# Reordering the first step of a Strassen-Winograd MLP: an operand split ahead of the up products, other roundings behind a copy

## The chip, the cores and the metric

The kernel runs on one core of a Trainium2 chip. The metric is device microseconds for one execution, the median of several runs. The core's engines are named PE (TensorE, the matmuls), ACT (ScalarE), DVE (VectorE), POOL (GpSimd) and SP (SyncE, which issues most DMAs). Each works through its own list of instructions in order; semaphores tie the lists together.

## The reference

A trunk of two layers on 512 tokens of width 1024. Layer 0 mixes with multi-head latent attention, layer 1 with gated linear attention; behind each stands an MLP of hidden width 4096 with a squared ReLU. The change touches the MLPs alone:

```
def sq_relu_mlp(xn, w_up, w_down):
    hid = jnp.square(jax.nn.relu(xn @ w_up))
    return hid @ w_down

x = x + sq_relu_mlp(rms_norm(x, norm_mlp[i]), w_up[i], w_down[i])
```

All values are float32, x is 512x1024, w_up 1024x4096 and w_down 4096x1024.

## The kernel before, in words

**Products in three matmuls.** To keep float32 accuracy every operand is split into a high part, rounded to the format that PE multiplies at full speed (an ACT instruction), and a low part, the rest (a DVE instruction): `split`, lines 124 and 127; with a sign, `signed`, lines 870 and 871. A product is then high x high, high x low and low x high. Tiles `wh` and `wl` are the parts of weights and rotate over four buffers each.

**The MLP.** `mlp` is called once per layer; `nxt` is set in the first MLP (a norm follows) and empty in the second. The hidden width is cut into eight blocks of 512. `up_first` makes the first block with plain products. Then seven calls of `step(b, ...)` follow, each of which makes the next hidden block (up) and adds the present one to the result (down). Both are 2x2 block products done with seven instead of eight quadrant products (Strassen-Winograd), so sums and differences of quadrants have to be formed first: of x once (`quadrants`, tiles T), of the weights in each step (in place, tiles `wraw` and `comb`, or by an accumulating DMA of POOL), of the hidden block in each step (`q11` to `q22`). A hidden block's quadrants lie in tiles that the trace calls `set`; their parts lie in `hidden_parts` in the first MLP and in `set` tiles in the second. There are four rooms for such parts (`parts_room`), used in turn.

**One step in its order on PE.** Up: products named by their x operand, "11" into bank z, T1 into w, T2 onto z, "21" onto y, T3 onto z, "22" onto w, T4 onto z. Between them ACT copies banks: y is a copy of z behind "11" (T2 may overwrite z only then), w2 a copy of w behind T1, u a copy of z behind T2, v a copy of z behind T3. `finish` (lines 885 and 886) applies ReLU and square to a finished quadrant. Down: d11 into the pair of banks d, whose sum ACT copies to the pair e; then d22, d12 (onto e), d11 again (onto d), dS1, d12, dS3. A product `onto` a total starts by copying ("seeding") the total from SBUF into two `u` banks. Up products are line 993; down products are line 1006 in the first MLP and line 1013 in the second.

**The operands of the down products.** In step 0, before the change: q11 is split ahead of the up products (`p11`). Behind the copy e of d11 in the source come, in this order, q12 = q22 - q12 (L1067), q11 = q11 + q12 (L1068), the parts of q21 (`p21`, for the first d12), q21 = q21 - q11 (L1070) and its negated parts (for d22), then the negated parts of the new q11 (for the second d11), and the parts of q22 (`p22`, for the second d12).

**The totals.** The residual stream itself serves as the totals S11, S12, S21 and SU. `residual` prepares it: in the first MLP it negates SU in place (L931, ACT) and forms the difference S21 (L932, DVE); in the second it first turns the tiles by transpositions on PE (L941) through d and e, which ACT copies out (L945, L946, L948) before DVE forms S21 (L949). The third transposition needs the bank that L945 frees.

**What sets the order.** The Tile framework orders each engine's instructions by its own estimate of when they can run, from the order in the source and the dependencies; `tc.issue_after(i)` keeps instructions behind instruction i, and `tc.keep_in_program_order` keeps one at its place in the source.

Of the kernel before, what the change touches and what calls it, by code (L numbers as in the profile page):

```python
# [14 lines left out]
AF = mybir.ActivationFunctionType  # L15
ALU = mybir.AluOpType
# [34 lines left out]
def trunk_kernel(ctx: ExitStack, tc: tile.TileContext, t_in: dict, out: bass.AP):  # L51
    nc = tc.nc
    PE, ACT, DVE, POOL, SP = nc.tensor, nc.scalar, nc.vector, nc.gpsimd, nc.sync
# [5 lines left out]
    def uname(s):  # L59
        count[0] += 1  # L60
        return f"{s}_{count[0]}"
# [17 lines left out]
    def two_banks(tag):  # L79
        return psum["pool"].tile([P, 1024], F32, tag=f"ps_{tag}", bufs=1, name=uname("ps2"))  # L80
# [8 lines left out]
    def tmp(shape=(P, 512), dt=F32):  # L89
        return sb.tile(list(shape), dt, tag="tmp", bufs=6, name=uname("tmp"))  # L90
# [739 lines left out]
    def mlp(layer, nrm, nxt=None):  # L830
# [20 lines left out]
        if nxt:  # L851
            S11, S12, S21, SU = (xall[:, c * KH : (c + 1) * KH, t] for c in range(2) for t in (first, second))
        else:
            S11, S12, SU, S21 = (xall[:, 2 * i : 2 * i + 2].rearrange("p a t -> p (a t)") for i in range(4))
# [18 lines left out]
        def parts_of_quad(src, sign=1.0):  # L873
            hi, lo = parts_room[turn[0] % 4]
            turn[0] += 1
            if sign == 1.0:
                split(src, hi, lo)
            else:
                signed(src, hi, lo, sign)
            return hi, lo  # L880

        def finish(src, half, th, q):
            r = tmp()
            r_t = nrm.rstd[:, (first, second)[th]].unsqueeze(1).to_broadcast([P, 2, TH])
            DVE.scalar_tensor_tensor(by_tile(r), by_tile(src), 0.0, r_t, ALU.min if half else ALU.max, ALU.mult)
            ACT.activation(q[half][th], r, AF.Square)
# [40 lines left out]


        def residual():
            if nxt:  # L930
                ACT.activation(SU, SU, AF.Copy, scale=-1.0)  # L931
                DVE.scalar_tensor_tensor(S21, S21, -1.0, SU, ALU.mult, ALU.subtract)  # L932
                return

            def turned(tag, c, th):
                p = two_banks(tag)
                for t in range(2):
                    for j in range(4):
                        o = t * 512 + j * P
                        src = xT[4 * c + j][:, th * TH + t * P : th * TH + (t + 1) * P]  # L940
                        PE.matmul(p[:, o : o + P], src, ident, start=j == 0, stop=j == 3, is_transpose=True, skip_group_check=True)  # L941
                return p

            p, q = turned("d", 0, 0), turned("e", 0, 1)
            ACT.activation(S11, p, AF.Copy)  # L945
            ACT.activation(S12, q, AF.Copy)  # L946
            p, q = turned("d", 1, 1), turned("e", 1, 0)
            ACT.activation(SU, p, AF.Copy, scale=-1.0)  # L948
            DVE.scalar_tensor_tensor(S21, q, -1.0, SU, ALU.mult, ALU.subtract)  # L949
# [66 lines left out]
        def step(b, q, r, after):  # L1016
            (q11, q12), (q21, q22) = q
            A1, A2, s1 = W["A1"], W["A2"], W["S1"]
            a11, a12, s3, a22 = A1[:, :KH], A1[:, KH:], A2[:, :KH], A2[:, KH:]
            d11, d12, ds1, ds3, d22 = (W[n] for n in ("d11", "d12", "dS1", "dS3", "d22"))  # L1020

            def copied(dst, src):
                ACT.activation(dst, src, AF.Copy)  # L1023
                return dst

            def onto(total, a, parts, fresh=False):
                pair = [bank("u"), bank("u")]
                cols = [part_of(total, i) for i in range(2)]
                if not fresh:
                    for p, c in zip(pair, cols):  # L1030
                        copied(laid(p), c)
                down_product(pair, a, parts, fresh)
                for p, c in zip(pair, cols):
                    copied(c, laid(p))

            p11 = None if b else parts_of_quad(q11)
            w, w2, z, y = (bank("u") for _ in range(4))
            up_product(z, a11, "11", True)
            copied(y, z)
            DVE.tensor_tensor(a11, s1, a11, ALU.add)  # L1040
            up_product(w, s1, "T1", True)
            copied(w2, w)
            after("S1")
            up_product(z, a11, "T2", False)
            u = copied(tmp(), z)
            up_product(y, a12, "21", False)
            finish(y, 0, 0, r)
            DVE.tensor_tensor(a12, a11, a12, ALU.add)
            up_product(z, s3, "T3", False)
            v = copied(tmp(), z)  # L1050
            c = tmp()
            DVE.tensor_tensor(c, w2, v, ALU.add)
            finish(c, 1, 1, r)
            up_product(w, a12, "22", False)
            c = tmp()
            DVE.tensor_tensor(c, w, u, ALU.add)
            finish(c, 0, 1, r)
            after("A1")
            up_product(z, a22, "T4", False)
            finish(z, 1, 0, r)  # L1060
            after("A2")

            d = two_banks("d")
            down_product(d, d11, p11 or parts_of_quad(q11), True)
            e = copied(two_banks("e"), d)
            DVE.tensor_tensor(d11, ds1, d11, ALU.add)
            DVE.tensor_tensor(q12, q22, q12, ALU.subtract)  # L1067
            DVE.tensor_tensor(q11, q11, q12, ALU.add)  # L1068
            p21 = parts_of_quad(q21)
            DVE.tensor_tensor(q21, q21, q11, ALU.subtract)  # L1070
            onto(S21, d22, parts_of_quad(q21, -1.0))
            after("d22")
            down_product(e, d12, p21, False)
            DVE.tensor_tensor(S11, laid(e), S11, ALU.add)
            down_product(d, d11, parts_of_quad(q11, -1.0), False)
            e = copied(two_banks("e"), d)
            DVE.tensor_tensor(d12, d11, d12, ALU.add)
            after("d11")
            p22 = parts_of_quad(q22)
            DVE.tensor_tensor(q22, q22, q11, ALU.subtract)  # L1080
            onto(S5, ds1, parts_of_quad(q22, -1.0), b == 0)
            after("dS1")
            down_product(e, d12, p22, False)
            DVE.tensor_tensor(S12, laid(e), S12, ALU.add)
            after("d12")
            down_product(d, ds3, parts_of_quad(q12), False)
            DVE.tensor_tensor(SU, laid(d), SU, ALU.add)
            after("dS3")

        up_first(Q[0])  # L1090
        quadrants()
        residual()
        for name in ("A1", "S1", "A2", "d11", "dS1", "d22", "d12", "dS3"):
            fetch(0, name)
        last_raw, last, gain = [], [[], []], []
# [43 lines left out]
        if nxt:  # L1139
# [7 lines left out]
            for c in range(2):  # L1147
                if c == 0:
                    ps_ = [bank("u") for _ in range(4)]
                else:  # L1150
                    e, d = split_banks("e"), split_banks("d")
# [541 lines left out]
    O, begun = mla(0, nrm, w0, mla_pools)  # L1693
# [25 lines left out]
    Y, begun = gla(0, n_mix1, "B", "B")  # L1719
# [54 lines left out]
```

## Time and profile before

| | |
|---|---|
| median of 3 runs | 1041.1 us (1040.84 to 1041.17) |
| the profiled execution | 1041.6 us, its span 1039.9 us |
| DVE busy / ACT busy | 878.8 us (85%) / 695.8 us (67%) |
| granted PE clock | 0.998 |
| first step of the first MLP | 206.0 to 245.1 us of the span |
| first step of the second MLP | 740.4 to 782.5 us |

The span runs from the first to the last instruction of the profiled execution; the execution's own time contains 1.7 us around it. Rows of a timeline give start and duration in us, engine, line of the source, operation, output and input tile (numbers left out), shapes, a count if several were merged, and in brackets the idle time of the engine before it with what ended it. Rows of windows give the stretch, its length, and for each engine its busy time and, in brackets, the number of instructions; then the granted clock, the share of time in which the DMA engines worked, and GB/s.

### The profile page before, as it was taken

The page shows a single profiled execution, that of the slowest core. Times are in us where ns is not written, and L with a number is a line of the kernel's source. Part 1 is how long each engine was busy: PE and PEld are TensorE (multiplying, and loading weights), DVE is VectorE, ACT ScalarE, POOL GpSimd, SP SyncE. Part 2 cuts the span into 40 slices and gives each one's busy share as a digit, 9 for nine tenths or more (in the row PEclk, how much of TensorE's full clock was granted, in tenths as well). Part 3 has the DMA queues.
Part 4 walks back from the last instruction along what each step waited for, and adds up shares of the span by engine and source line. Part 5 has one row for each costly group of instructions (what it writes and reads, how often), then busy time and mean ns, then how long its engine had stood idle before and what let it go on. Part 6 is the DMA issues. An engine that isn't in the chain of part 4 may idle for free.

```text
span 1039.9 us, 16853 instructions
## 1 busy us (share of the span) xinstructions
PE 1028.7 (99%) x6522; PEld 922.0 (89%) x6522; DVE 878.8 (85%) x1343; ACT 695.8 (67%) x1130; POOL 113.6 (11%) x128
## 2 busy tenths in 40 slices
PE   9999999999999999999999999999999999999997
PEld 7788888899999999998888888888989989989986
DVE  7889976999989989989686499469699999898994
ACT  8667754586776876775345565655577687677785
POOL 7400000411111111000000000000001101111000
PEclk9999999999999999999999999999999999999999
DMA  7401214788788778623313212164678778778522
GB/s 234 123 21 41 82 41 151 194 203 197 188 204 203 182 200 204 146 82 122 91 41 95 95 55 82 50 160 150 151 185 197 177 208 198 188 195 191 121 82 82
DMA packets 120001, 145.85 MB, mean 140 GB/s; under 512 B 9488, under 2 KB 86288, under 8 KB 119920
## 3 DMA queue, kind: packets, MB, share of 16 engines
q1 hardware_dynamic: 95424, 113.57, 34.2%
q0 software_dynamic: 22400, 29.36, 18.1%
q10 hardware_dynamic: 2096, 1.84, 0.6%
q8 instruction: 51, 0.84, 0.3%
q14 instruction: 30, 0.25, 0.1%
HBM read 142.39 MB, written 2.10 MB: 139 GB/s over the span
## 4 chain that ended last, share of the span: by engine, by line
PE 88%; DVE 5%; ACT 3%; DMA 2%; issue 1%; SPq 0%; ACTq 0%; DVEq 0%
PE ps L993 26%; PE ps L1013 13%; PE ps L1006 12%; PE ps L132 10%; PE ps L134 10%; PE ps L133 10%; PE ps L1413 1%; PE ps L149 1%; PE ps L1193 1%; DVE wl L127 1%; DMA wraw<-in_mla_w_in_dram 1%; PE ps L1540 1%; ACT wh L124 1%; DVE acc L266 1%; PE ps L1159 1%
## 5 line engine op out<-in xcount | busy, mean ns | idle before, releaser
L124 ACT ACTIVATE wh<-wraw 128x1024 fp32r<-128x1024 f32 x139 | 146.3, 1056 | 118.5 <-issue 39.7
L127 DVE TENSOR_TENSOR wl<-wraw,wh 128x1024 fp32r<-128x1024 f32 x139 | 169.7, 1222 | 38.4 <-ACT wh L124 37.7
L993 PE MATMUL ps<-T,wh 128*128 128x256 f32 x896 | 154.6, 275 | 0.6 <-ACT tmp L1023 0.6
L127 DVE TENSOR_TENSOR wl<-comb,wh 128x1024 fp32r<-128x1024 f32 x112 | 136.7, 1221 | 14.2 <-ACT wh L124 14.2
L124 ACT ACTIVATE wh<-comb 128x1024 fp32r<-128x1024 f32 x112 | 118.4, 1058 | 41.3 <-issue 31.4
L993 PEld LDWEIGHTS ps<-T,wh 128*128 128x128 f32 x896 | 134.7, 188 | 0.8 <-ACT tmp L1023 0.8
L1013 PE MATMUL ps<-wh,set 128*128 128x512 f32 x392 | 122.3, 390 | 1.4 <-ACT ps L1023 1.4
L993 PE MATMUL ps<-T,wl 128*128 128x256 f32 x448 | 123.3, 275 | 0.0
L993 PE MATMUL ps<-set,wh 128*128 128x256 f32 x672 | 116.7, 276 | 0.0
L132 PE MATMUL ps<-set,wh 128*128 128x512 f32 x280 | 109.5, 391 | 0.0
L133 PE MATMUL ps<-set,wh 128*128 128x512 f32 x280 | 109.5, 391 | 0.0
L134 PE MATMUL ps<-set,wl 128*128 128x512 f32 x280 | 109.3, 390 | 0.0
L1006 PE MATMUL ps<-hidden_parts,wh 128*128 128x256 f32 x784 | 105.9, 275 | 0.0
L993 PEld LDWEIGHTS ps<-set,wh 128*128 128x128 f32 x672 | 101.6, 188 | 0.5
L1006 PEld LDWEIGHTS ps<-hidden_parts,wh 128*128 128x128 f32 x784 | 96.7, 188 | 0.0
L993 PE MATMUL ps<-set,wl 128*128 128x256 f32 x336 | 92.6, 276 | 0.0
L1013 PEld LDWEIGHTS ps<-wh,set 128*128 128x128 f32 x392 | 73.6, 188 | 17.2 <-ACT ps L1023 1.8
L993 PEld LDWEIGHTS ps<-T,wl 128*128 128x128 f32 x448 | 84.1, 188 | 0.0
L1013 PE MATMUL ps<-wl,set 128*128 128x512 f32 x196 | 76.1, 389 | 0.0
L993 PEld LDWEIGHTS ps<-set,wl 128*128 128x128 f32 x336 | 63.1, 188 | 0.0
L134 PEld LDWEIGHTS ps<-set,wl 128*128 128x128 f32 x280 | 52.6, 188 | 11.2 <-DVE wl L127 0.2
L133 PEld LDWEIGHTS ps<-set,wh 128*128 128x128 f32 x280 | 52.6, 188 | 10.9 <-DVE set L765 0.2
(405 smaller groups left out, 2213.1 us busy)
## 6 DMA issues: line engine op xcount, KB each, us to landing
comb<-in_mlp_w_down_dram SPq DMA_DIRECT2D x74, 512.0 KB, 4.5
wraw<-in_mlp_w_up_dram SPq DMA_DIRECT2D x18, 1024.0 KB, 5.6
wraw<-in_mlp_w_up_dram SPq DMA_DIRECT2D x28, 512.0 KB, 5.8
comb<-in_mlp_w_down_dram POOLq DMA_DIRECT2D x28, 512.0 KB, 6.7
wraw<-in_gla_w_in_dram SPq DMA_DIRECT2D x12, 1024.0 KB, 5.2
comb<-in_mlp_w_up_dram SPq DMA_DIRECT2D x14, 512.0 KB, 4.7
comb<-in_mlp_w_up_dram POOLq DMA_DIRECT2D x14, 512.0 KB, 6.2
wraw<-in_mlp_w_up_dram POOLq DMA_DIRECT2D x14, 512.0 KB, 7.8
```

Of the source, the lines that this page charges most:

```text
L124: order(ACT.activation(hi, src, AF.Copy))
L127: lo_eng.tensor_tensor(lo, src, f(hi), ALU.subtract)
L132: PE.matmul(psum, wh, xh, start=start, stop=False)
L133: PE.matmul(psum, wh, xl, start=False, stop=False)
L134: PE.matmul(psum, wl, xh, start=False, stop=stop)
L149: PE.transpose(psum, src, ident[: src.shape[0], : src.shape[0]])
L266: DVE.tensor_tensor(self.acc, self.acc, s, ALU.add)
L993: PE.matmul(o, a_, x_, start=start and j == 0 and k == 0 and n == 0, stop=k == KH - 1 and n == 2, skip_group_check=True)
L1006: PE.matmul(o, w_[:, k, j * P : (j + 1) * P], x_[:, ts], start=opens, stop=k == 1 and n == 2, skip_group_check=True)
L1013: PE.matmul(o, x_, w_, start=start and k == 0 and n == 0, stop=k == 1 and n == 2, skip_group_check=True)
L1159: PE.matmul(p, a, x, start=k == 0 and n == 0, stop=k == 3 and n == 2)
L1193: PE.matmul(o, a, b_, start=False, stop=k == 3 and n == 2, skip_group_check=True)
```

## The change

Five edits, all in `mlp`. They concern step 0 alone (`b == 0`), and there differ between the two MLPs:

1. The parts of q21 (`p21`) are made ahead of the up products, behind those of q11.
2. In the second MLP the two sums of quadrants (`combined`) and the negated q21 with its parts (`negated`) are made there too.
3. In the second MLP the negated parts of q11 and the parts of q22 are issued behind the first copy e (`later`).
4. In the first MLP `residual` is no longer called before the steps; its two instructions stand in step 0 behind the sum for the "22" quadrant (lines 1067 and 1068 of the new file), the DVE one held at its place in the source.
5. The copy e of d11 is written out as `begun`, so that edit 3 can name it.

```diff
         def residual():
-            if nxt:
-                ACT.activation(SU, SU, AF.Copy, scale=-1.0)
-                DVE.scalar_tensor_tensor(S21, S21, -1.0, SU, ALU.mult, ALU.subtract)
-                return
...
-            p11 = None if b else parts_of_quad(q11)
+            def combined():
+                DVE.tensor_tensor(q12, q22, q12, ALU.subtract)
+                DVE.tensor_tensor(q11, q11, q12, ALU.add)
+
+            def negated():
+                DVE.tensor_tensor(q21, q21, q11, ALU.subtract)
+                return parts_of_quad(q21, -1.0)
+
+            p11, p21, m21 = None, None, None
+            if b == 0:
+                p11 = parts_of_quad(q11)
+                p21 = parts_of_quad(q21)
+                if not nxt:
+                    combined()
+                    m21 = negated()
...
             DVE.tensor_tensor(c, w, u, ALU.add)
+            if nxt and not b:
+                ACT.activation(SU, SU, AF.Copy, scale=-1.0)
+                tc.keep_in_program_order(DVE.scalar_tensor_tensor(S21, S21, -1.0, SU, ALU.mult, ALU.subtract))
             finish(c, 0, 1, r)
...
-            e = copied(two_banks("e"), d)
+            e = two_banks("e")
+            begun = ACT.activation(e, d, AF.Copy)
+
+            def later():
+                return nullcontext() if b or nxt else tc.issue_after(begun.ins)
+
             DVE.tensor_tensor(d11, ds1, d11, ALU.add)
-            DVE.tensor_tensor(q12, q22, q12, ALU.subtract)
-            DVE.tensor_tensor(q11, q11, q12, ALU.add)
-            p21 = parts_of_quad(q21)
-            DVE.tensor_tensor(q21, q21, q11, ALU.subtract)
-            onto(S21, d22, parts_of_quad(q21, -1.0))
+            if not m21:
+                combined()
+                p21 = p21 or parts_of_quad(q21)
+                m21 = negated()
+            onto(S21, d22, m21)
             after("d22")
             down_product(e, d12, p21, False)
             DVE.tensor_tensor(S11, laid(e), S11, ALU.add)
-            down_product(d, d11, parts_of_quad(q11, -1.0), False)
+            with later():
+                m11 = parts_of_quad(q11, -1.0)
+            down_product(d, d11, m11, False)
...
-            p22 = parts_of_quad(q22)
+            with later():
+                p22 = parts_of_quad(q22)
...
         quadrants()
-        residual()
+        if not nxt:
+            residual()
```

The lists of POOL and SP stay as they were, instruction by instruction; those of PE, ACT and DVE change in the two first steps only, but for a few neighbours that change places in the second MLP's step 1.

**ACT, first MLP, step 0, around the copies y, w2 and u.** In these rows `ps_2369<-ps_2368` is the copy y of z, `ps_2367<-ps_2366` is w2, `tmp_2460<-ps_2368` is u; `set_2150` is q21 and `set_2148` q11; `wh_2462` belongs to a12, `wh_2494` to S3, `wh_2529` to the new a12. Before:

```order
L124 ACTIVATE wh_2462<-wraw_2343 128x1024
L1023 ACTIVATE ps_2369<-ps_2368 128x512
L124 ACTIVATE wh_2494<-wraw_2348 128x1024
L124 ACTIVATE hidden_parts<-set_2150 128x512
L870 ACTIVATE hidden_parts<-set_2148 128x512
L1023 ACTIVATE ps_2367<-ps_2366 128x512
L124 ACTIVATE wh_2529<-wraw_2343 128x1024
L124 ACTIVATE wh_2564<-wraw_2348 128x1024
L1023 ACTIVATE tmp_2460<-ps_2368 128x512
```

Now (`wh_2566` is before's `wh_2564`, a22's high part, and L1018 is before's L1023):

```order
L124 ACTIVATE wh_2462<-wraw_2341 128x1024
L902 ACTIVATE set_2150<-tmp_2303 128x256
L902 ACTIVATE set_2151<-tmp_2303 128x256
L124 ACTIVATE hidden_parts<-set_2150 128x512
L124 ACTIVATE wh_2494<-wraw_2346 128x1024
L1018 ACTIVATE ps_2369<-ps_2368 128x512
L124 ACTIVATE wh_2529<-wraw_2341 128x1024
L1018 ACTIVATE ps_2367<-ps_2366 128x512
L870 ACTIVATE hidden_parts<-set_2150 128x512
L870 ACTIVATE hidden_parts<-set_2148 128x512
L124 ACTIVATE wh_2566<-wraw_2346 128x1024
L1018 ACTIVATE tmp_2460<-ps_2368 128x512
```

The high part of q21 (L124, from `set_2150`) and S3's rounding have moved ahead of the copy y, and both negated parts (L870) stand between the copies w2 and u; before, one of them stood behind u.

**ACT, first MLP, step 0, around the copy v.** `tmp_2522<-ps_2368` is v, `ps_2638<-xT` and `ps_2639<-xT` are the seeds of d22, `set_2152` and `set_2155` are squares, `wh_2642` is d22's high part. Before:

```order
L124 ACTIVATE wh_2600<-comb_2352 128x1024
L886 ACTIVATE set_2152<-tmp_2490 128x512
L1023 ACTIVATE ps_2638<-xT 128x512
L124 ACTIVATE wh_2642<-comb_2357 128x1024
L1023 ACTIVATE tmp_2522<-ps_2368 128x512
L124 ACTIVATE wh_2674<-comb_2359 128x1024
L886 ACTIVATE set_2155<-tmp_2526 128x512
L1023 ACTIVATE ps_2639<-xT 128x512
```

Now:

```order
L124 ACTIVATE wh_2602<-comb_2350 128x1024
L886 ACTIVATE set_2152<-tmp_2490 128x512
L124 ACTIVATE wh_2642<-comb_2355 128x1024
L1018 ACTIVATE tmp_2522<-ps_2368 128x512
L124 ACTIVATE wh_2674<-comb_2357 128x1024
L886 ACTIVATE set_2155<-tmp_2526 128x512
L1018 ACTIVATE ps_2638<-xT 128x512
L1018 ACTIVATE ps_2639<-xT 128x512
```

Both seeds now stand behind v and the square `set_2155`; before, one stood two places ahead of v.

**PE, second MLP, step 0, at the end of the first down product.** `ps_1350` is the pair d and `ps_1353` the pair e, `ps_8366` is a seeded bank of d22; `set_7853` is q21's high part, `set_7855` and `set_7856` are the negated parts. Before:

```order
L1013 MATMUL ps_1350_8339<-wl_8341,set_7851 128x512
L1013 MATMUL ps_1350_8339<-wh_8340,set_7852 128x512
L1013 MATMUL ps_1353_8356<-wh_8390,set_7853 128x512
L1013 MATMUL ps_1353_8356<-wl_8391,set_7853 128x512
L1013 MATMUL ps_1353_8356<-wh_8390,set_7854 128x512
```

Now:

```order
L1008 MATMUL ps_1350_8346<-wl_8348,set_7851 128x512
L1008 MATMUL ps_1350_8346<-wh_8347,set_7852 128x512
L1008 MATMUL ps_8366<-wh_8370,set_7855 128x512
L1008 MATMUL ps_8366<-wl_8371,set_7855 128x512
L1008 MATMUL ps_8366<-wh_8370,set_7856 128x512
```

Behind d11 stood the first matmuls of d12, onto e; now d22 stands there, all twelve matmuls of it, and d12 follows.

At the start of the same step the high part of q21 (`set_7853`) now stands on ACT directly ahead of the copy of the first transposition (L945, L940 in the new file), and PE's third transposition (L941, now L936) stands behind ten matmuls of "11" instead of eight.

## The prediction

> **What bounds the kernel now.** I read the page first, then all waits of TensorE (PE), then windows over the two stages that the diff touches, then the timelines of ScalarE (ACT) and VectorE (DVE) there.
>
> ```profile
> span 1039.9 us, 16853 instructions
> ...
> PE 1028.7 (99%) x6522; PEld 922.0 (89%) x6522; DVE 878.8 (85%) x1343; ACT 695.8 (67%) x1130; POOL 113.6 (11%) x128
> ```
>
> PE has work in flight for 99% of the span, so an edit of orders on ACT and DVE can return only what PE loses by waiting. The waits of PE, as "line waited for: us in total, times, longest", hold two that lie in the stages of this change:
>
> ```profile
> PE ps L1013 <- ACT ps L1023: 1.4, 1, 1.4
> PE ps L1680 <- DVE ones L195: 1.2, 1, 1.2
> PE ps L993 <- ACT tmp L1023: 0.6, 1, 0.6
> ```
>
> The first is in the second MLP (L1013 are its down products), the third in the first MLP (up products, L993); the second is at the start of the program. What each really costs is read by comparing a stage with its twin. Each window below runs from the first matmul of seven products to the first one behind them: up products of the first MLP in step 0 and in step 1, then down products of the second MLP in step 0 and in step 1. The first number behind the window is its length.
>
> ```profile
> 206.04:226.03 19.99, 19.43 (x170) 19.24 (x169) 19.33 (x23) 14.01 (x21) 2.51 (x2) 1.00 0.75 187
> 245.07:264.11 19.04, 19.04 (x171) 19.04 (x170) 16.95 (x20) 12.72 (x18) 3.80 (x3) 1.00 0.85 221
> 761.60:782.49 20.89, 19.48 (x87) 15.61 (x86) 19.53 (x25) 16.54 (x24) 1.34 (x2) 1.00 0.64 161
> 801.57:820.65 19.08, 19.08 (x87) 15.77 (x86) 18.11 (x21) 15.30 (x22) 1.46 (x2) 1.00 0.72 177
> ```
>
> The matmuls are the same in number, and step 1 has no gap: a product takes 19.04 / 7 = 2.72 us. So step 0 loses 19.99 - 19.04 = 0.95 us in the first MLP and 20.89 - 19.08 = 1.81 us in the second. **The ceiling of the change is 2.76 us**, 0.27% of 1041 us. It also shows that DVE is busy for 19.33 of the 19.99 us: in the first MLP nothing can be moved on DVE without moving what stands behind it.
>
> **The first MLP, the wait that goes.** ACT, then PE, then DVE, each by start, duration and (in brackets) the idle time before:
>
> ```profile
> 208.28 1.06 ACT L124 ACTIVATE wh<-wraw 128x1024 fp32r<-128x1024 f32 x1 [3.92 <-DVE wraw L1040]
> 209.25 0.70 ACT L902 ACTIVATE set<-tmp 128x256 f32<-128x256 f32 x2
> 209.86 1.05 ACT L124 ACTIVATE wh<-wraw 128x1024 fp32r<-128x1024 f32 x1
> 210.81 0.58 ACT L1023 ACTIVATE ps<-ps 128x512 f32<-128x512 f32 x1
> ...
> 220.52 0.63 ACT L886 ACTIVATE set<-tmp 128x512 f32<-128x512 f32 x1 [1.35 <-DVE tmp L885]
> 221.06 0.58 ACT L1023 ACTIVATE ps<-xT 128x512 f32<-128x512 f32 x1
> 221.58 1.05 ACT L124 ACTIVATE wh<-comb 128x1024 fp32r<-128x1024 f32 x1
> 222.54 0.58 ACT L1023 ACTIVATE tmp<-ps 128x512 f32<-128x512 f32 x1
> ```
>
> ```profile
> 211.49 0.45 PE L993 MATMUL ps<-T,wh 128*128 128x256 f32 x2
> 223.16 0.50 PE L993 MATMUL ps<-T,wh 128*128 128x256 f32 x2 [0.56 <-ACT tmp L1023]
> 223.51 0.28 PE L993 MATMUL ps<-T,wl 128*128 128x256 f32 x1
> ```
>
> ```profile
> 202.96 1.21 DVE L932 SCALAR_TENSOR_TENSOR xT<-xT 128x1024 f32<-128x1024 f32 x1
> ...
> 206.97 1.22 DVE L1040 TENSOR_TENSOR wraw<-comb,wraw 128x1024 f32<-128x1024 f32 x1
> 208.10 0.68 DVE L900 SCALAR_TENSOR_TENSOR tmp<-ps,rstd 128x512 f32<-128x512 f32 x1
> ...
> 219.81 0.68 DVE L885 SCALAR_TENSOR_TENSOR tmp<-ps,rstd 128x512 f32<-128x512 f32 x1
> 220.41 1.22 DVE L127 TENSOR_TENSOR wl<-comb,wh 128x1024 fp32r<-128x1024 f32 x1
> ```
>
> T4 goes into the bank that T3 filled, so it waits for the copy v (222.54 to 223.12, then PE at 223.16). T2 began at 211.49 and T3 is the second product behind it, so T3 ended at 211.49 + 3 x 2.72 = 219.65; the copy was late only because of what stands ahead of it on ACT: a square that waited for L885 on DVE (219.81 + 0.68 = 220.49), a seed copy and a weight rounding. The change takes L932 (1.14 us of DVE) out of the time before L885, and the seed copy (0.52 on ACT) from before v. That alone brings v forward by 1.66 us, more than the 0.95 lost in the whole stage.
>
> **The first MLP, the waits that come.** The second operand's rounding now stands ahead of two copies that PE also needs. I follow the new order with the durations above, and these slots from start to start: 1.14 for a DVE instruction of 1024 elements and 0.60 for one of 512 (206.97 to 208.10, 219.81 to 220.41), 0.96 for an ACT rounding of 1024 (221.58 to 222.54), 0.53 for an ACT instruction of 512 (220.52 to 221.58 are two), 0.35 for half a square.
> - DVE, from 202.96: a11's low part, q11's low part, then the sum a11+S1 at 202.96 + 1.14 + 0.60 = 204.70, ended 1.22 later at 205.92. ACT then rounds the sum at 206.01 (before at 208.28) and a12 at 206.97.
> - DVE: low part of S1 at 205.83, of the sum at 207.09 (it needs ACT's 206.01 + 1.06), L900 at 208.23 to 208.91, a12's low part at 208.83, the difference q22-q12 at 209.97, q21's low part at 210.57, the sum for a12 at 211.17 to 212.39.
> - ACT: two half squares at 208.95, the new high part of q21 at 209.66, S3's rounding at 210.20, and only then the copy y at 211.16 to 211.74 (before 210.81 to 211.39). T2 needs y's bank: it starts at 211.77 in place of 211.49, 0.28 later, and pays about 0.06 more for the restart.
> - ACT goes on: rounding of the new a12 at 212.48 (after DVE's 212.39), the copy w2 at 213.44. The negated q21 needs q21-q11, on DVE behind S3's low part (212.31) and the sum q11 (213.45): 214.05 to 214.73. So ACT does the two negated parts at 214.78 and 215.32, a22's rounding at 215.86 and the copy u at 216.82 to 217.40. T3 could start at 211.77 + 0.06 + 2 x 2.72 = 217.27 and starts at 217.44: about 0.17, and some 0.1 for the restart (at 223.16 two matmuls took 0.35 to the next start; an undisturbed pair takes 0.23).
> - Then v: L885 ends at 218.8, the square at 219.4, the rounding of d22 follows the end of T3 at 220.4, v is done by 222.0, and T4 wants it at 223.0. One microsecond to spare.
>
> New waits 0.28 + 0.06 + 0.17 + 0.1 = 0.61. **First MLP: 0.95 - 0.61 = 0.34 us won.** The residual difference (L1068 of the new file) runs on DVE after "22" has ended (223.0) and is done by 224.5; the two seeds follow on ACT until 226.5. PE reaches d22 at about 228.4, so 1.9 us cover it. The copy e comes later on ACT than the seeds, two squares, one weight rounding and one operand rounding; I get its end at 230.2 and its need at 231.1. If that cover went, PE would wait there for what is missing. Bounds for this stage: 0.95 won if neither copy makes PE wait; nothing won if the chain to y runs 0.34 later than here.
>
> **The second MLP.** The end of d11 on PE and the matmul behind it, then ACT around it:
>
> ```profile
> 764.13 0.39 PE L1013 MATMUL ps<-wh,set 128*128 128x512 f32 x1
> 765.92 0.50 PE L1013 MATMUL ps<-wh,set 128*128 128x512 f32 x1 [1.41 <-ACT ps L1023]
> ```
>
> ```profile
> 739.71 0.72 ACT L902 ACTIVATE set<-tmp 128x256 f32<-128x256 f32 x2
> 740.51 1.03 ACT L945 ACTIVATE xT<-ps 128x1024 f32<-128x1024 f32 x1
> ...
> 746.32 0.58 ACT L1023 ACTIVATE ps<-ps 128x512 f32<-128x512 f32 x1
> ...
> 763.75 1.21 ACT L124 ACTIVATE set<-set 128x512 fp32r<-128x512 f32 x2
> 764.86 1.01 ACT L1023 ACTIVATE ps<-ps 128x1024 f32<-128x1024 f32 x1
> ```
>
> Before, PE runs d12 first, because the negated operand of d22 isn't there, and d12 adds to a copy e of d11 that can only start when d11 has ended. After, the negated operand exists before the up products, and PE has d22 (2.72 us) between d11 and d12. The copy takes 1.01 and starts at about 764.8, while d12 then wants it at 764.36 + 2.72 = 767.1: 1.2 us of cover. All 1.81 us go.
>
> What is paid: the high part of q21 (0.53) now stands before L945 on ACT, which frees the bank of the third transposition:
>
> ```profile
> 741.24 0.40 PE L993 MATMUL ps<-set,wh 128*128 128x256 f32 x2
> 741.59 2.00 PE L941 MATMUL ps<-ident,xT 128*128 128x128 f32 x16
> ```
>
> L945 ended at 740.51 + 1.03 = 741.54 and PE went on at 741.59, 0.12 after the two matmuls at 741.24 would have let it (741.47). With the rounding ahead, L945's successor runs from 740.97 to 742.00. The new order puts two more matmuls (0.23) ahead of the transposition, so PE is ready at 741.70 and goes on at 742.05: 0.35 of wait in place of 0.12, so 0.23 lost. The copy y (746.32) has 0.85 to spare against its T2, and later rounding waits (m11, p22 behind the copy) end more than 1 us ahead of their products. **Second MLP: 1.81 - 0.23 = 1.58 us won**; bounds 1.1 (the 0.85 of cover missed by half) and 1.81.
>
> **The sum.** 0.34 + 1.58 = 1.92 us. No DMA, no instruction of GpSimd or SyncE and no matmul count changes, and the roundings are only moved, so nothing is added elsewhere. The profiled execution took 1041.6 us (its span and 1.7 around it); the median of the runs is 1041.1. From that: 1041.1 - 1.9 = **1039.2 us**. 0.2%, about what a measurement of this kernel can tell from no change, is 2.08 us, just beyond this.
>
> [...] In both stages with the waits the windows show a granted clock of 1.00, and the seven products of each add up to step 1's time plus the waits. [...]
>
> **The rivals.**
> - *Both copies of the first MLP come in time.* For it: the waits that I find there are 0.28 and 0.17 at the end of chains of a dozen instructions. Against it: DVE is busy for 19.33 of 19.99 us there. 0.95 + 1.58 = 2.53 us won, 1038.6. Chance 0.22.
> - *DVE is one slot later there.* Every link up to y and u goes over DVE, and one more slot of 1024 elements ahead of the sum a11+S1 makes the wait of T2 1.14 longer. 1.92 - 1.14 = 0.78 won, 1040.3. Chance 0.14.
> - *Slower: ACT stands behind DVE's q21-q11 in both MLPs.* ACT runs in order, and the negated part of q21 now stands before y or u. If DVE is late by L, the first MLP loses L, and the second what L exceeds the 0.85 of y's cover by. The whole gain is gone from L = 1.4 (1.92 = 1.4 + 0.55). With three slots, L = 3.4: 3.4 + 2.55 - 1.92 = 4.0 slower, 1045.1. Against it: L932's slot is given back to DVE exactly there. Chance 0.06.
> - That the change doesn't do what it says is excluded by the order of instructions: PE does d22 behind d11.
>
> **The numbers.** The forecast keeps 0.55, with a range of its own of 1038.8 to 1039.8 (first MLP 0 to 0.6 won, second 1.3 to 1.7). About 0.3 of it lies beyond 2.08 us won. Faster by over 0.2%: 0.55 x 0.3 + 0.19 of the first rival = 0.36. Slower: 0.06 + 0.02 of the clock's = 0.08. Within: 0.56. The range takes in the ceiling (1041.1 - 2.76 = 1038.3) and the late slot of DVE with a little beyond it (1040.5), and leaves out the slower cases.
>
> **What would show it.** Right: in the second MLP no wait of PE for the copy e, d22 behind d11, a window of down products of 19.1 us, and a wait near 0.35 at the third transposition; in the first MLP no wait at T4, but short ones at T2 and T3, and a window near 19.65. Wrong: a window of the first MLP of 19.05 (the first rival) or above 20, PE waiting for e or for the seeds, or a granted clock below 1.00.

## The result and the profile after

The changed kernel takes 1039.16 us (median of 15 runs, 1038.46 to 1040.04) against 1041.17 (15 runs, 1040.84 to 1041.73): ratio 0.9979, 95% interval 0.9972 to 0.9987. That is 2.0 us, just under the 2.08 that make 0.2%. The profiled execution of the changed kernel took 1039.75 us:

```profile
span 1038.0 us, 16859 instructions
...
PE 1028.6 (99%) x6522; PEld 922.3 (89%) x6522; DVE 879.2 (85%) x1343; ACT 694.5 (67%) x1130; POOL 111.9 (11%) x128
```

PE's busy time is what it was (1028.7 before, 1028.6 now); the span is 1.9 us shorter. So PE waits less, and the waits of PE name what went (waits as short as those at T2 and T3 below don't stand in this view):

```profile
PE ps L1701 <- DVE ones L195: 1.2, 1, 1.2
PE ps L436 <- ACT set L276: 0.8, 2, 0.6
PE ps L692 <- ACT pr L143: 0.4, 2, 0.2
PE ps L132 <- DVE set L511: 0.2, 1, 0.2
PE ps L1434 <- DVE A L1446: 0.2, 1, 0.2
```

Neither the 1.4 us of the down products (for the copy e) nor the 0.6 of the up products (for v) is there any more. The wait of L436 has grown by 0.5; it lies in the first 10 us of the program, where the change touches nothing, and is taken up at the end. The same windows as in the prediction, each from the first matmul of a stage to the first of the next: up products of the first MLP in step 0, transpositions with the up products of the second MLP, its down products. The fourth row is the middle one's counterpart in the kernel before:

```profile
206.52:226.17 19.65, 19.53 (x170) 19.23 (x168) 19.21 (x23) 13.38 (x19) 1.73 (x2) 1.00 0.80 200
738.67:761.58 22.91, 22.86 (x201) 22.60 (x200) 18.25 (x21) 15.87 (x22) 1.81 (x2) 1.00 0.62 152
761.58:780.66 19.08, 19.08 (x86) 15.78 (x85) 18.23 (x22) 15.04 (x21) 2.39 (x2) 1.00 0.70 171
```

```profile
738.78:761.60 22.82, 22.82 (x202) 22.61 (x201) 16.53 (x18) 14.96 (x20) 2.10 (x2) 1.00 0.64 153
```

The first MLP won 19.99 - 19.65 = 0.34, the second won 20.89 - 19.08 = 1.81 and paid 22.91 - 22.82 = 0.09: 2.06 us in all, beside 2.0 between the medians. The stage of the first MLP began 206.52 - 206.04 = 0.48 later in this execution than in that of before, ahead of all that changed. The stretch from its up products to the first transposition took 738.67 - 226.17 = 512.50 in place of 738.78 - 226.03 = 512.75; of what changed it holds the first MLP's down products of step 0, which took 19.04 in both.

PE around the starts of T2 (212.04) and T3 (217.87) in the first MLP of the changed kernel:

```profile
211.87 0.28 PE L988 MATMUL ps<-T,wl 128*128 128x256 f32 x1
212.04 0.50 PE L988 MATMUL ps<-T,wh 128*128 128x256 f32 x2
212.38 0.28 PE L988 MATMUL ps<-T,wl 128*128 128x256 f32 x1
...
217.48 0.28 PE L988 MATMUL ps<-set,wl 128*128 128x256 f32 x1
217.87 0.51 PE L988 MATMUL ps<-T,wh 128*128 128x256 f32 x2
218.21 0.28 PE L988 MATMUL ps<-T,wl 128*128 128x256 f32 x1
```

An undisturbed single matmul is followed by the next after 0.11, an undisturbed pair after 0.23. T2 started 0.17 behind its predecessor, so it waited 0.06; T3 0.39 behind, so it waited 0.28. After each, the pair took 0.34 in place of 0.23: the restart costs 0.11 beyond the wait. ACT there:

```profile
211.40 0.58 ACT L1018 ACTIVATE ps<-ps 128x512 f32<-128x512 f32 x1
...
215.24 1.16 ACT L870 ACTIVATE hidden_parts<-set 128x512 fp32r<-128x512 f32 x2 [0.86 <-DVE set L1036]
216.30 1.04 ACT L124 ACTIVATE wh<-wraw 128x1024 fp32r<-128x1024 f32 x1
217.25 0.57 ACT L1018 ACTIVATE tmp<-ps 128x512 f32<-128x512 f32 x1
...
221.83 0.57 ACT L1018 ACTIVATE tmp<-ps 128x512 f32<-128x512 f32 x1
```

T2 waits for y (ended 211.98), T3 for u (ended 217.82): u stands behind a22's rounding, and that behind the two negated parts, for which ACT stood idle for 0.86 until DVE had formed q21 - q11 (L1036). The copy v (221.83) is done a microsecond before T4 wants it.

### The profile page after: what moved, and what is told of

Same layout as the page of the kernel before. It is cut to its first block, busy times and chain, and to the rows that moved or that the text cites. A ratio compares the mean times of both kernels' runs of the same rounds, so it can differ in the third digit from the quotient of the medians.

```text
span 1038.0 us, 16859 instructions
## 1 busy us (share of the span) xinstructions
PE 1028.6 (99%) x6522; PEld 922.3 (89%) x6522; DVE 879.2 (85%) x1343; ACT 694.5 (67%) x1130; POOL 111.9 (11%) x128
## 4 chain that ended last, share of the span: by engine, by line
PE 92%; DVE 4%; ACT 2%; DMA 1%; issue 1%; SPq 0%; ACTq 0%; DVEq 0%
PE ps L988 25%; PE ps L1008 13%; PE ps L1001 13%; PE ps L132 10%; PE ps L133 10%; PE ps L134 10%; PE ps L1180 2%; PE ps L149 1%; PE ps L1434 1%; PE ps L1214 1%; PE ps L1561 1%; DVE wl L127 1%; PE ps L436 1%; DMA xT<-in_x_dram 1%; ACT wh L124 1%
## 5 line engine op out<-in xcount | busy, mean ns | idle before, releaser
L124 ACT ACTIVATE wh<-wraw 128x1024 fp32r<-128x1024 f32 x139 | 146.1, 1056 | 114.2 <-PE ps L133 37.6
L124 ACT ACTIVATE wh<-comb 128x1024 fp32r<-128x1024 f32 x112 | 118.6, 1059 | 43.3 <-issue 30.0
L132 PE MATMUL ps<-set,wh 128*128 128x512 f32 x280 | 109.6, 391 | 0.0
```

The costliest lines, as they stand in the source:

```text
L124: order(ACT.activation(hi, src, AF.Copy))
L132: PE.matmul(psum, wh, xh, start=start, stop=False)
```

## The experiments

A pair of windows is compared in each: the up products of the first MLP ("first window": 19.99 before, 19.65 after) and the down products of the second ("second window": 20.89 before, 19.08 after). They are steadier than the whole time.

**e1: the second MLP alone.** The diff against the changed kernel: the early split only where no norm follows, the residual difference back ahead of the steps.

```diff
-                p21 = parts_of_quad(q21)
                 if not nxt:
+                    p21 = parts_of_quad(q21)
...
-            if nxt and not b:
-                ACT.activation(SU, SU, AF.Copy, scale=-1.0)
-                tc.keep_in_program_order(DVE.scalar_tensor_tensor(S21, S21, -1.0, SU, ALU.mult, ALU.subtract))
...
             residual()
+        else:
+            ACT.activation(SU, SU, AF.Copy, scale=-1.0)
+            DVE.scalar_tensor_tensor(S21, S21, -1.0, SU, ALU.mult, ALU.subtract)
```

Expected:

> The change in the second MLP alone; the first MLP is as before. If the two MLPs simply add up, as the prediction has it: the seven down products of the second MLP in step 0 take 19.08 us (20.89 before), its transpositions and up products 22.91 (as after; 22.82 before), the seven up products of the first MLP 19.99, and the time is 1041.17 - 1.81 + 0.09 = 1039.4 us. Rival, that what the second MLP wins is partly given back further on (say in the stage behind its down products): the window still shows 19.08, but the time stays above 1040.3, half of it gone.

Measured: 1039.78 us beside 1041.42 of the kernel before on the same chip, ratio 0.9985, interval 0.9976 to 0.9994. The two windows:

```profile
205.35:225.40 20.05, 19.50 (x170) 19.27 (x169) 19.39 (x23) 14.02 (x21) 2.53 (x3) 1.00 0.78 193
761.15:780.23 19.08, 19.08 (x87) 15.77 (x86) 18.23 (x22) 15.05 (x21) 1.76 (x2) 1.00 0.71 172
```

1041.42 - 1.81 + 0.09 = 1039.70 is what adding up gives. Nothing is given back further on; the second MLP is by far the larger part.

**e2: the first MLP alone.** The diff:

```diff
-                p21 = parts_of_quad(q21)
-                if not nxt:
-                    combined()
-                    m21 = negated()
+                if nxt:
+                    p21 = parts_of_quad(q21)
...
-                return nullcontext() if b or nxt else tc.issue_after(begun.ins)
+                return nullcontext()
```

Expected:

> The change in the first MLP alone; the second MLP is as before. Adding up: the seven up products of the first MLP 19.65 us (19.99 before), the down products of the second 20.89, the time 1041.17 - 0.34 = 1040.8 us, within 0.2% of before and hardly to be told from it in time; the window decides. Rival, that the first MLP's part costs or wins nothing: window 19.9 to 20.1 and 1041.2.

Measured: 1041.15 us beside 1041.42, ratio 0.9997, interval 0.9989 to 1.0006. The time can't tell it from no change, as said; the windows can:

```profile
206.17:225.86 19.69, 19.61 (x169) 19.29 (x168) 19.23 (x23) 13.43 (x19) 3.13 (x3) 1.00 0.85 212
761.22:782.08 20.86, 19.45 (x87) 15.61 (x85) 19.52 (x25) 16.55 (x24) 1.38 (x2) 1.00 0.67 159
```

0.30 won in the first window, and the second is as before. With e1, 1.64 + 0.27 = 1.91 us by the medians: the two halves add up.

**e3: in the first MLP the residual difference late, but the split of q21 behind d11 again in the source.**

```diff
-                p21 = parts_of_quad(q21)
                 if not nxt:
+                    p21 = parts_of_quad(q21)
```

Expected:

> In the first MLP only the residual difference stays late; the second down operand is split where it was before, behind d11. The second MLP has the whole change. If it is the residual difference's DVE and ACT work that made T4 wait, and the early split that makes T2 and T3 wait: the wait at T4 is gone and nearly none comes for it, window of the first MLP 19.05 to 19.3 us (19.65 after), time 1038.6 to 1038.8. Rival, that the early split is needed there too (something else keeps T4 waiting): window at or above 19.65, time 1039.2 or more.

Measured: 1039.87 us beside 1041.42, ratio 0.9985, interval 0.9976 to 0.9994. The first window, PE at T3, and ACT from the part of q21 to the copy u:

```profile
206.02:225.76 19.74, 19.49 (x170) 19.26 (x168) 19.21 (x23) 13.26 (x19) 2.51 (x2) 1.00 0.74 183
```

```profile
216.93 0.28 PE L988 MATMUL ps<-set,wl 128*128 128x256 f32 x1
217.45 0.50 PE L988 MATMUL ps<-T,wh 128*128 128x256 f32 x2 [0.25 <-ACT tmp L1018]
```

```profile
209.37 0.62 ACT L124 ACTIVATE hidden_parts<-set 128x512 fp32r<-128x512 f32 x1
...
210.84 0.58 ACT L1018 ACTIVATE ps<-ps 128x512 f32<-128x512 f32 x1
213.35 0.64 ACT L870 ACTIVATE hidden_parts<-set 128x512 fp32r<-128x512 f32 x1 [1.92 <-DVE set L1033]
213.89 1.05 ACT L124 ACTIVATE wh<-wraw 128x1024 fp32r<-128x1024 f32 x1
214.84 0.58 ACT L1018 ACTIVATE ps<-ps 128x512 f32<-128x512 f32 x1
215.35 0.62 ACT L870 ACTIVATE hidden_parts<-set 128x512 fp32r<-128x512 f32 x1
...
216.82 0.57 ACT L1018 ACTIVATE tmp<-ps 128x512 f32<-128x512 f32 x1
```

My theory fell by half. The wait at T4 is gone with the split behind d11 in the source, and the first matmul of T2 starts on time; but T3 waits 217.45 - 216.93 - 0.11 = 0.41, more than in the changed kernel, and the window is no shorter.

What the split does to T2 this run can't tell. The scheduler put the high part of q21 ahead of the copy y in this kernel too (209.37), and up to y ACT's list is that of the changed kernel: y ends 210.84 + 0.58 - 206.02 = 5.40 behind the start of the stage here and 211.40 + 0.58 - 206.52 = 5.46 there. Of the split only the low part, on DVE, stands further back. e4 and e5 below answer that question.

T3's wait comes from elsewhere. The rows show it: the scheduler put the negated part of q11 ahead of the rounding of the new a12, and ACT stood idle for 1.92 us until DVE had formed q11 (L1033). What stood behind it waited too, the copy u among it. (The medians show 1.55 won where the windows give 1.98; the rest lies within the spread of the program's start, told at the end.)

On ACT a ready instruction didn't pass the waiting one in this trace: the new a12's rounding runs here 213.89 - 206.02 = 7.87 us behind the start of the stage, and 5.68 in e5 below, where no waiting instruction stands ahead of it; the sum that it rounds ends at 5.56 here and at 5.59 there.

**e4: the split early, but the residual difference where it was.** The edits of e1 to `residual` alone, in the first MLP. Expected:

> In the first MLP the second down operand is split early, but the residual difference stays where it was, ahead of the steps; the second MLP has the whole change. If DVE's order is what sets the copies y and u there: T2 waits about 0.5 and T3 about 1.1 us, the window of the first MLP is near 20.8 us (19.99 before, 19.65 after), the time 1039.2 + 1.2 = 1040.4. Rival, that the split ahead is harmless and its waits in the changed kernel come from elsewhere: window 19.65 or less, or 19.99 with the old wait at T4, time 1039.2 to 1039.5.

Measured: 1040.65 us beside 1041.42, ratio 0.999, interval 0.9981 to 0.9999.

```profile
206.53:227.15 20.62, 19.66 (x170) 19.27 (x168) 19.96 (x23) 14.61 (x21) 2.52 (x3) 1.00 0.77 199
```

The window is 0.63 longer than before the change: PE's starts show 0.26 of wait at T2 and 1.02 at T3 (0.5 and 1.1 were expected), with 0.15 and 0.13 of restart. So the early split alone would have made the first MLP slower; the late residual difference pays for it. At T2 this is the price of the split itself: with q21's high part ahead of it, y ends 211.62 + 0.58 - 206.53 = 5.67 behind the start of the stage, and 210.81 + 0.58 - 206.04 = 5.35 before the change. The granted clock stays at 1.00 with both waits in the stage.

**e6: one more slot of DVE ahead of the steps in the first MLP.** Its result is overwritten later.

```diff
             p11, p21, m21 = None, None, None
+            if nxt and not b:
+                for _ in range(1):
+                    tc.keep_in_program_order(DVE.scalar_tensor_tensor(S5, S21, -1.0, S21, ALU.mult, ALU.subtract))
```

Expected:

> The changed kernel with one more VectorE instruction of 1024 elements ahead of the steps in the first MLP (its result is overwritten later). If, as the prediction's rival prices it, every link up to y and u goes over VectorE: the waits of T2 and T3 together grow by 1.14 us, the first window from 19.65 to about 20.8, the time to 1040.3. If ScalarE alone sets them (VectorE has slack): the window grows by less than 0.4.

Measured: 1040.33 us beside 1041.47, ratio 0.9989, interval 0.9980 to 0.9998.

```profile
205.97:226.63 20.66, 19.66 (x169) 19.27 (x168) 20.00 (x23) 13.70 (x19) 2.44 (x3) 1.00 0.79 197
```

```profile
206.75 1.22 DVE L1052 TENSOR_TENSOR wraw<-comb,wraw 128x1024 f32<-128x1024 f32 x1
```

The window grew by 20.66 - 19.65 = 1.01 us for one slot of 1.14; PE waits 0.32 at T2 and 1.00 at T3. The prediction's rival put the 1.14 at T2; most of it arrives at T3, by way of the sums that the negated parts wait for. But this isn't the slot alone: the sum a11+S1 (the row) starts 206.75 - 205.97 = 0.78 behind the start of the stage, and in the changed kernel 206.52 - 205.03 = 1.49 ahead of it. That is two slots later and not one, since the scheduler also put a low part before the sum, and on ACT it put the negated part of q11 ahead of the copy w2. This is the order of e4, whose window is 20.62. So the 1.01 is what the slot costs with the order that the scheduler made of it.

**e7: the later roundings not held behind the copy of the first sum.**

```diff
-                return nullcontext() if b or nxt else tc.issue_after(begun.ins)
+                return nullcontext()
```

Expected:

> The changed kernel without the hold of the later roundings (the negated q11 and q22) behind the copy of the first sum in the second MLP. If d22 between d11 and d12 covers the copy, as the prediction has it: the copy ends up to 1.1 us later, within its 1.2 us of cover, the down window stays at 19.08 to 19.2 us and the time at 1039.2. Rival, that holding those roundings is what keeps TensorE from waiting: a wait near 1 us for the copy e returns, window near 20.1, time 1040.2.

Measured: 1039.36 us beside 1041.47, ratio 0.998, interval 0.9971 to 0.9989. The second window, and the copy e on ACT here and in the changed kernel:

```profile
761.08:780.16 19.08, 19.08 (x87) 15.77 (x86) 18.38 (x22) 15.19 (x22) 1.19 (x1) 1.00 0.74 176
```

```profile
764.34 1.01 ACT L1078 ACTIVATE ps<-ps 128x1024 f32<-128x1024 f32 x1
```

```profile
764.54 1.01 ACT L1078 ACTIVATE ps<-ps 128x1024 f32<-128x1024 f32 x1 [0.71 <-PE ps L1008]
```

Counted from the start of the stage the copy comes at 764.34 - 761.08 = 3.26 in place of 764.54 - 761.58 = 2.96: only 0.30 later, not 1.1, since the two roundings fill the 0.71 us in which ACT stands idle in the changed kernel. With d22 behind d11 the copy is covered either way. This part of the change, which the title names, does nothing for the time here.

**e8: in the second MLP the split early, the negated operand not.**

```diff
                 p21 = parts_of_quad(q21)
-                if not nxt:
-                    combined()
-                    m21 = negated()
```

Expected:

> In the second MLP only the split of the second down operand stands ahead of the up products; the combination and the negated operand stand behind the copy of the first sum in the program, and are placed by the scheduler. TensorE does d22 behind d11 in this order too. If the order of TensorE (d22 between d11 and d12) wins the 1.81 us, and not how early the negated operand exists: d22 waits at most 0.5 us for its high part, the down window is 19.1 to 19.6 us, the time 1039.2 to 1039.7. Rival, that the negated operand must exist before the up products: d22 waits for VectorE's difference and the low part, over 1 us, window above 20.1, time above 1040.2.

Measured: 1039.92 us beside 1041.47, ratio 0.9984, interval 0.9975 to 0.9993.

```profile
760.95:780.65 19.70, 19.55 (x86) 15.62 (x85) 19.26 (x23) 15.70 (x22) 1.19 (x1) 1.00 0.74 166
```

```profile
764.57 0.39 PE L1008 MATMUL ps<-wl,set 128*128 128x512 f32 x1
765.11 0.73 PE L1008 MATMUL ps<-wh,set 128*128 128x512 f32 x2
```

Of 1.81 us, 20.89 - 19.70 = 1.19 come already with d22 ahead of d12 in PE's order, which the scheduler chooses in this kernel too; the other 0.62 need the negated operand earlier. They are short waits with their restarts, the longest at 765.11: 0.54 behind the matmul before it in place of 0.23, when DVE had just ended the negated low part (765.05). So the negated operand need not exist before the up products; that it need only be there when d11 ends follows from these rows, though no run places it just there.

**e5: all copies first.** From e3: in the first MLP the split of q21 and both negated operands stand behind the copy u on ACT. In the second MLP the split of q21 stands behind the copies of the turned tiles. Against the changed kernel:

```diff
-            ACT.activation(S12, q, AF.Copy)
+            turned_out.append(ACT.activation(S12, q, AF.Copy))
...
-                p21 = parts_of_quad(q21)
                 if not nxt:
+                    with tc.issue_after(turned_out[0].ins):
+                        p21 = parts_of_quad(q21)
                     combined()
...
-            u = copied(tmp(), z)
+            u = tmp()
+            taken = ACT.activation(u, z, AF.Copy)
...
             if not m21:
-                combined()
-                p21 = p21 or parts_of_quad(q21)
-                m21 = negated()
+                with nullcontext() if b else tc.issue_after(taken.ins):
+                    combined()
+                    p21 = p21 or parts_of_quad(q21)
+                    m21 = negated()
...
-            with later():
+            with tc.issue_after(taken.ins) if nxt and not b else later():
                 m11 = parts_of_quad(q11, -1.0)
```

Expected:

> Beside the changed kernel: in the first MLP the split of the second down operand and both negated operands stand behind the copy u on ScalarE (the combination stays where VectorE has room), the residual difference stays late; in the second MLP the split of the second down operand stands behind the copies of the turned tiles, the rest of the change is there. If ScalarE's order ahead of y and u is all that is left in the first MLP: no wait at T2, T3 or T4, window 19.04 to 19.1 us (19.65 after); the transpositions and up products of the second MLP 22.82 (22.91 after), its down products 19.08; time 1039.2 - 0.6 - 0.1 = 1038.5 us. Rival, that VectorE's own load (busy nearly the whole stage) sets the copies whatever ScalarE's order: a wait remains at T3 or T4 or comes at d22, the first window stays at or above 19.5, and the time at 1039.1 or more.

Measured: 1038.88 us (1038.73 to 1038.95) beside 1041.47, ratio 0.9973, interval 0.9962 to 0.9984. The windows (up and down products of the first MLP, transpositions with up products of the second) and ACT at the rounding of the new a12, at u and at the first part behind u:

```profile
206.25:225.31 19.06, 19.06 (x170) 19.06 (x169) 18.07 (x22) 13.59 (x19) 2.51 (x2) 1.00 0.79 192
225.31:244.50 19.19, 19.19 (x171) 19.14 (x169) 19.12 (x22) 16.00 (x23) 3.04 (x3) 1.00 0.77 191
737.90:760.72 22.82, 22.82 (x202) 22.60 (x201) 18.32 (x21) 16.06 (x22) 2.47 (x2) 1.00 0.65 153
```

```profile
211.93 1.07 ACT L124 ACTIVATE wh<-wraw 128x1024 fp32r<-128x1024 f32 x1 [0.77 <-PE ps L990]
...
215.53 0.58 ACT L1058 ACTIVATE tmp<-ps 128x512 f32<-128x512 f32 x1
216.00 0.63 ACT L124 ACTIVATE hidden_parts<-set 128x512 fp32r<-128x512 f32 x1
```

No wait at T2, T3 or T4 is left: 19.06 beside step 1's 19.04. With no part of q21 ahead of it, y ends 210.58 + 0.58 - 206.25 = 4.91 us behind the start of the stage, in e3 5.40. The copy u runs at 9.28, in e3 at 10.80 (216.82 - 206.02), and the only difference between the two sources in the first MLP is the hold behind u. DVE was no later in e3: its list is the same in both up to the sum q11, which ends at 7.29 there and at 7.33 here. That shows the cause of T3's wait in e3: ACT's order, which put an instruction that waits for this sum ahead of u. In the changed kernel the rows show the same kind of wait, for q21 - q11. The third transposition costs nothing more (22.82). Some 0.15 is given back in the first MLP's down products (19.19 in place of 19.04), one of whose matmuls starts 0.11 late.

**e9 and e10: the changed kernel and e5's side by side.** Both unaltered, on one chip. Expected:

> The changed kernel unaltered, so that it stands beside the next kernel on the same chip. Windows as in its first trace: first MLP 19.64 us, transpositions and up products of the second MLP 22.91, its down products 19.08; median near 1039.2 to 1039.4.

> The kernel with all copies first, unaltered, on the same chip as the changed kernel. By the windows it should be 0.53 us faster than that (0.59 in the first MLP's up products, 0.09 at the third transposition, less 0.15 in the first MLP's down products): 1038.7 to 1038.9. Rival, that the windows don't add up to the time: a median within 0.2 us of the changed kernel's.

Measured: the changed kernel 1039.61 us (1038.69 to 1040.06; ratio 0.9978, interval 0.9970 to 0.9987), e5's 1038.80 (1038.47 to 1039.43; ratio 0.9973, interval 0.9962 to 0.9983), the kernel before 1041.74. First windows, that of the changed kernel above:

```profile
206.61:226.41 19.80, 19.65 (x169) 19.25 (x168) 19.36 (x22) 13.55 (x19) 2.51 (x2) 1.00 0.75 190
```

```profile
205.62:224.68 19.06, 19.06 (x170) 19.06 (x169) 18.15 (x22) 13.67 (x19) 1.96 (x2) 1.00 0.79 189
```

The medians lie 0.81 apart, but the single runs overlap and so do the two intervals, so the times alone don't settle it. The windows do: 19.80 - 19.06 = 0.74 in the up products of the first MLP in these two executions, of which e5's kernel gives back 0.14 in the down products behind them; with 22.91 - 22.83 = 0.08 at the third transposition that makes 0.68, where 0.53 was expected. The changed kernel's own window isn't steady, 19.65 in one execution and 19.80 in the other; T2 waited 0.06 there and 0.22 here. A kernel with spare time ahead of its copies has 19.06 in both.

## Why the prediction was right, point by point

- *The ceiling of 2.76 us.* It holds. e5 wins 0.93 in the first window and 1.81 in the second and gives back 0.15, 2.59 in all, and its median lies 1041.47 - 1038.88 = 2.59 below that of before.
- *The wait at T4 goes, since the residual difference leaves DVE and ACT.* Right: with the residual difference early it stays (e1: window 20.05), with it late it goes without the split ahead of the up products in the source (e3). In e4 it is early and T4 doesn't wait, but there T3 started 1.02 late. Which of the two does it, the DVE instruction that left or the seed copy on ACT, these runs don't separate.
- *New waits in the first MLP of 0.28 + 0.06 at T2 and 0.17 + 0.1 at T3, 0.61 in all, window 19.65.* The sum and the window came out (19.65), the terms only roughly: 0.06 + 0.11 at T2 and 0.28 + 0.13 at T3. The chain to y was 0.24 later than forecast by the clock (211.40 for 211.16), but the stage itself began 0.48 later, so T2 waited less; the copy u was forecast for 216.82 and came at 217.25, 0.43 later, nearly the whole shift. T3 starts when u has landed, whatever T2 lost before, so the time of u decides the sum: 10.78 behind the start of the stage was forecast (216.82 - 206.04), 10.73 came. That a chain so long fits so well is partly luck: in the second trace of the same kernel u comes at 10.89, and the window is 19.80.
- *DVE one slot later costs 1.14.* Near in size (e6: 1.01), but e6 changed the order on DVE and ACT as well, so the price of the slot alone stays open. The slot that L932 gave back was needed: e4, without it, is 0.63 slower in that stage than before the change.
- *ACT stands behind DVE's q21 - q11.* The rival's mechanism is real, only small: ACT stood 0.86 for L1036, of which T3 saw 0.28. In e3, where ACT stood 1.92 for q11, T3 saw 0.41. It never came near the 3.4 that the rival needed.
- *The second MLP: all 1.81 go.* Right (19.08), with the order of PE worth 1.19 and the early negated operand 0.62 (e8). The hold of the later roundings adds nothing (e7); the prediction gave it no price of its own.
- *The clock.* The forecast's 0.02 for a slower clock is a term that no run shows; in its place the granted clock was 1.00 in every window of every kernel above, those with two waits among them.
- *0.23 paid at the third transposition.* The mis-sized term: 0.09 was paid, and e5, with the split behind the copies, gets it back. ACT and PE there:

```profile
740.23 0.62 ACT L124 ACTIVATE set<-set 128x512 fp32r<-128x512 f32 x1
740.75 1.00 ACT L940 ACTIVATE xT<-ps 128x1024 f32<-128x1024 f32 x1
```

```profile
741.48 0.28 PE L988 MATMUL ps<-set,wh 128*128 128x256 f32 x1
741.81 2.00 PE L936 MATMUL ps<-ident,xT 128*128 128x128 f32 x16
```

PE waited 741.81 - 741.48 - 0.11 = 0.22, not 0.35. The copy moved by 0.35, counted from the first transposition (740.75 - 738.67 = 2.08; before 740.51 - 738.78 = 1.73), not by the 740.97 - 740.51 = 0.46 of the forecast, nor by the whole 0.53 of the rounding: before, ACT already stood idle for some 0.18 ahead of it (740.51 - 739.71 is 0.80 where two half squares take 0.62), and the rounding filled that.

Forecast were 1.92 us; the three stages give 2.06, and the 0.14 between them is that one term.

## What to carry to other kernels

Before moving work out of the way of a bank's copy, ask which instruction ahead of that copy waits for another engine, since what was ready behind it here waited as well: in e3 the new a12's rounding by 7.87 - 5.56 = 2.31 us. Where a matmul has to wait for a copy of what PE has just made, look for an independent product to put between the two: here one of 19.08 / 7 = 2.73 us (d22) hid a copy of 1.01 (e) whole, and its operand need only have been there when d11 ended, as the rows of e8 suggest (no run placed it there). For edits worth a few tenths of a microsecond, compare the stage with its undisturbed twin in one trace: 0.3 us out of 20 is plain there and can't be seen in the time.

## What the runs showed that I had not expected

The time of this kernel varies in its first 17 us. PE's first products wait for gain-scaled tiles of x (L276): 0.3 us in the profiled execution of before, 0.8 in that of the changed kernel, and 1.5 in its second trace (first row). ACT makes those tiles and itself waits for weights and gains from memory there (from the changed kernel's first trace):

```profile
PE ps L436 <- ACT set L276: 1.5, 2, 1.0
```

```profile
4.77 0.72 ACT L276 ACTIVATE set<-xT,gains 128x512 fp32r<-128x512 f32 x1 [0.39 <-DMA gains<-in_gains_dram]
...
7.71 0.63 ACT L124 ACTIVATE wh<-wraw_ckv 128x512 fp32r<-128x512 f32 x1 [1.29 <-DMA wraw_ckv<-in_mla_w_in_dram]
```

The first matmul behind those products (L132) starts 16.52 us into the span in e1 and 17.78 in e9, and the start of the first MLP's up products spreads by the same 1.26, from 205.35 (e1) to 206.61 (e9). That is nearly four times what the change wins in the first MLP; no edit here touches that stretch.

A wait of PE for a bank cost more than the wait at T2 and T3 of these runs: the pair of matmuls behind it took 0.34 in place of 0.23, and those that followed started up to 10 ns later each, 0.11 to 0.16 in all per wait. The cost hardly depended on the length of the wait: T2 of the changed kernel waited 0.06 and lost 0.11 more, T3 of e4 waited 1.02 and lost 0.13 more. It even came without a wait: in e3 the first matmul of T2 starts on time (211.48, y had ended at 211.42), and its pair still takes 0.33. Why it comes no run shows.
